# The first block of a streaming row sum, loaded in two halves by two queues

## The chip, the cores and the metric

The kernel runs on one core of a Trainium2 chip. SyncE, VectorE and ScalarE are engines of the core, each with its own stream of instructions. SyncE and ScalarE can issue loads; a load waits in the queue of the engine that issued it, and 16 DMA engines carry it out in packets. The metric is the device time of one execution in microseconds (us), as the median of several runs. The kernel before took 162.17 us in three runs.

## The reference

```python
x = np.random.randn(32, 512, 1024).astype(np.float32)   # 67.1 MB
return (np.sum(x, axis=-1) * 0.5).astype(np.float32)    # 16,384 sums
```

Each of the 16,384 rows of 1024 numbers is summed and halved. Every byte of the input is read once, and there is very little arithmetic per byte.

## The kernel before

The rows are spread over 128 partitions, 128 rows to each, and worked on in eight blocks of 16 rows (8.39 MB a block). Three buffers hold blocks in the on-chip memory. SyncE issues all loads, VectorE sums a block with one instruction, and in the last two blocks ScalarE takes some of the rows.

```python
x_pool = ctx.enter_context(tc.tile_pool(name="x", bufs=3))
...
for b in range(n_blocks - 1):
    c0 = b * B
    t = x_pool.tile([P, B, D], fp32, name="xb")
    loads.append(nc.sync.dma_start(out=t, in_=x_rows[:, c0 : c0 + B, :]))
    h = B if b < n_blocks - 2 else B // 2
    nc.vector.reduce_sum(
        out=sums[:, c0 : c0 + h], in_=t[:, 0:h, :], axis=mybir.AxisListType.X
    )
    nc.vector.tensor_single_scalar(           # sums * 0.5 -> res
        ...
    )
    for r in range(h, B):
        act_row(t, r, c0 + r)
# ... the last block comes in five pieces, and its rows are shared out ...
```

A hook that runs when the program is complete moves SyncE's first loads in front of the entry barrier, where all engines meet before their work begins. With three buffers, these are the loads of blocks 0, 1 and 2. Each later load waits for the reduction that frees its buffer.

```python
def start_loads_at_entry(nc_):
    entry, *rest = nc_.main_func.blocks
    is_sp = lambda i: i.engine == mybir.EngineType.SP
    ...   # collect SyncE's leading loads that wait for nothing
    entry.instructions = head[:at] + lead + head[at:]
```

## Time and profile before

| what | value | from |
|---|---|---|
| span of the profiled run | 160.2 us | page |
| DMA engines, share of 16 engines' span | 97.4% | page, table of queues |
| VectorE busy | 119.3 us (74%) | page |
| start of the first, second, third reduction | 21.78, 41.11, 60.46 us | timeline |
| start of the very last VectorE sum | 157.55 us | chain |

The table is read in this order. The share of the DMA engines says that the transfers never rest. The starts of the reductions say how fast blocks arrive (19.3 us apart), and the first start says what is lost before the stream has its pace. What remains of the span after the last sum is the store of the last results.

The chain that ended last, in order of time, shows the same from the back. Its columns are start, duration and piece, and "..." stands for pieces that are left out:

```profile
0.43 40.66 DMA xb<-in_x_dram
...
41.11 17.23 DVE sums L96
...
58.36 40.78 DMA xb<-in_x_dram
...
118.24 39.23 DMA xb<-in_x_dram
...
157.55 0.45 DVE xb L80
```

Each DMA piece lasts 40 us although a block takes 19.3 us. A load lies in the queue behind another one for half of that time. So a reduction that is "on the chain" does not mean that the transfers waited for it.

### The profile page before, as it was taken

How to read it: one execution, taken by the hardware profiler on the slowest of the kernel's cores; microseconds unless marked ns; L12 is line 12 of the kernel's file. 1: busy time of each engine (PE TensorE's matmuls, PEld its weight loads, DVE VectorE, ACT ScalarE, POOL GpSimd, SP SyncE). 2: the span in 40 equal slices, each digit the busy share in tenths (PEclk: the TensorE clock that was granted, in tenths of full speed). 3: DMA queues.
4: the chain of work that ended last, by engine and by line, in shares of the span. 5: the costliest groups of instructions: out<-in, count | busy, mean ns of one | idle time of the engine just before them, and what ended most of it. 6: DMA issues, size and time to landing. Idle time of an engine off the chain costs nothing.

```text
span 160.2 us, 138 instructions
## 1 busy us (share of the span) xinstructions
DVE 119.3 (74%) x34; ACT 17.3 (11%) x31; POOL 0.2 (0%) x4
## 2 busy tenths in 40 slices
DVE  0000059997799969999599995999959999597443
ACT  0000000000000000000000000000000000599952
POOL 0000000000000000000000000000000000000000
DMA  7996996996996996997997998979969969999992
GB/s 278 507 524 262 524 524 262 524 524 262 524 524 262 524 524 262 524 475 311 524 442 344 524 409 376 524 311 475 524 278 507 524 278 507 393 393 425 430 399 72
DMA packets 2016, 67.18 MB, mean 419 GB/s; under 512 B 480, under 2 KB 608, under 8 KB 736
## 3 DMA queue, kind: packets, MB, share of 16 engines
q1 hardware_dynamic: 2016, 67.18, 97.4%
HBM read 67.11 MB, written 0.07 MB: 419 GB/s over the span
## 4 chain that ended last, share of the span: by engine, by line
DMA 75%; DVE 22%; SPq 1%; issue 0%; DVEq 0%
DMA xb<-in_x_dram 75%; DVE sums L96 22%; SPq L114 1%; DVE xb L80 0%; SPq L120 0%; SPq L94 0%; DVE res L99 0%; DVEq L205 0%
## 5 line engine op out<-in xcount | busy, mean ns | idle before, releaser
L96 DVE TENSOR_REDUCE sums<-xb 128x16 f32<-128x16384 f32 (+1 forms) x7 | 112.0, 16001 | 33.3 <-DMA xb<-in_x_dram 33.3
L70 ACT ACT_TABLE_LOAD x1 | 1.3, 1283 | 137.9 <-DMA xb<-in_x_dram 137.9
L70 ACT ACTIVATE xb<-xb 128x1024 f32<-128x1024 f32 x15 | 15.7, 1045 | 2.1 <-DMA xb<-in_x_dram 2.1
L80 DVE CUSTOM_DVE_ANT_0 xb<-xb 128x512 f32<-128x512 f32 (+1 forms) x9 | 5.6, 664 | 5.0 <-DMA xb<-in_x_dram 5.0
L70 ACT ACTIVATION_READ_ACCUMULATOR xb<-xb 128x1 f32 x15 | 2.8, 187 | 0.0
L99 DVE TENSOR_SCALAR res<-sums 128x16 f32<-128x16 f32 (+1 forms) x7 | 1.2, 174 | 0.2
L80 DVE DVE_READ_ACCUMULATOR2_ANT res<- 128x1 f32 x9 | 0.7, 83 | 0.0
L80 DVE CUSTOM_DVE_ANT_0 xb<-xb,part 128x224 f32<-128x224 f32 x1 | 0.5, 450 | 0.2 <-DMA xb<-in_x_dram 0.2
L191 POOL MEMSET const-bfloat16-1.0<- 128x1 bf16 x1 | 0.1, 101 | 0.0
L191 POOL MEMSET const-uint8-127<- 128x1 uint8 x1 | 0.1, 101 | 0.0
L191 POOL MEMSET const-float32-0.0<- 128x1 f32 x1 | 0.1, 98 | 0.2 <-issue 0.2
L191 POOL MEMSET const-float32-1.0<- 128x1 f32 x1 | 0.1, 98 | 0.0
L80 DVE DVE_READ_ACCUMULATOR2_ANT part<- 128x1 f32 x1 | 0.1, 83 | 0.0
## 6 DMA issues: line engine op xcount, KB each, us to landing
xb<-in_x_dram SPq DMA_DIRECT2D x1, 4096.0 KB, 31.1
xb<-in_x_dram SPq DMA_DIRECT2D x1, 2560.0 KB, 36.9
xb<-in_x_dram SPq DMA_DIRECT2D x1, 1024.0 KB, 38.9
xb<-in_x_dram SPq DMA_DIRECT2D x1, 288.0 KB, 39.1
xb<-in_x_dram SPq DMA_DIRECT2D x1, 224.0 KB, 39.2
xb<-in_x_dram SPq DMA_DIRECT2D x7, 40.8
out_dram<-res SPq DMA_DIRECT2D x1, 56.0 KB, 10.0
out_dram<-res SPq DMA_DIRECT2D x1, 8.0 KB, 1.4
```

Of the source, the lines that this page charges most:

```text
L70: acts.append(nc.scalar.activation(out=t[:, r, :], in_=t[:, r, :], func=mybir.ActivationFunctionType.Copy, scale=mul, accum_out=res[:, col ...
L80: return nc.vector.tensor_tensor_reduce(out=t[:, r, lo:mid], in0=t[:, r, lo:mid], in1=t[:, r, mid:hi], scale=mul, scalar=start, op0=ADD, o ...
L96: nc.vector.reduce_sum(out=sums[:, c0 : c0 + h], in_=t[:, 0:h, :], axis=mybir.AxisListType.X)
L99: nc.vector.tensor_single_scalar(out=res[:, c0 : c0 + h], in_=sums[:, c0 : c0 + h], scalar=mul, op=mybir.AluOpType.mult,)
L114: nc.sync.dma_start(out=t[:, lo:hi, :], in_=x_last[:, lo:hi, :])
L191: nc = _bacc.Bacc("TRN2", target_bir_lowering=False, num_devices=1)
```

## The change

The intent is to start the stream sooner: half of the first block is issued by ScalarE, whose queue stood idle, at the same time as SyncE issues the other half. Both go in front of the barrier.

```diff
     for b in range(n_blocks - 1):
         c0 = b * B
         t = x_pool.tile([P, B, D], fp32, name="xb")
-        loads.append(nc.sync.dma_start(out=t, in_=x_rows[:, c0 : c0 + B, :]))
+        if b == 0:
+            m = B // 2
+            loads.append(nc.sync.dma_start(out=t[:, 0:m, :], in_=x_rows[:, 0:m, :]))
+            loads.append(nc.scalar.dma_start(out=t[:, m:B, :], in_=x_rows[:, m:B, :]))
+        else:
+            loads.append(nc.sync.dma_start(out=t, in_=x_rows[:, c0 : c0 + B, :]))
...
+        for engine in (mybir.EngineType.SP, mybir.EngineType.Activation):
+            start_loads_of(nc_, engine)
+
+    def start_loads_of(nc_, engine):
         entry, *rest = nc_.main_func.blocks
-        is_sp = lambda i: i.engine == mybir.EngineType.SP
+        is_own = lambda i: i.engine == engine
...   # the rest of the hook uses is_own in place of is_sp
```

More of the change, by code (lines that the diff above doesn't have):

```diff
@@ L156, in start_loads_at_entry @@
             body = list(block.instructions)
-            own = [i for i in body if is_sp(i)]
+            own = [i for i in body if is_own(i)]
             if not any(is_load(i) for i in own):
@@ L168, in start_loads_at_entry @@
             at = next(
-                k for k, i in enumerate(head) if is_sp(i) and type(i).__name__ == "InstDrain"
+                k for k, i in enumerate(head) if is_own(i) and type(i).__name__ == "InstDrain"
             )
```

## The prediction

> **What bounds the kernel now.** I read the page first (busy shares, DMA queues, chain), then the timeline of VectorE, then the DMA view of the first 4 us, then the SyncE queue's waits.
>
> The page says that the transfers never rest, while VectorE has a quarter of the span free:
>
> ```profile
> DVE 119.3 (74%) x34; ACT 17.3 (11%) x31; POOL 0.2 (0%) x4
> ...
> q1 hardware_dynamic: 2016, 67.18, 97.4%
> ...
> DMA 75%; DVE 22%; SPq 1%; issue 0%; DVEq 0%
> ```
>
> The chain names VectorE for 22%, but that is how the walk back goes (a load waits for the reduction that frees its buffer), not a time in which the queue was empty. The timeline of VectorE settles it:
>
> ```profile
> 21.78 17.22 DVE L96 TENSOR_REDUCE sums<-xb 128x16 f32<-128x16384 f32 x1 [21.78 <-DMA xb<-in_x_dram]
> 39.03 0.17 DVE L99 TENSOR_SCALAR res<-sums 128x16 f32<-128x16 f32 x1
> 41.11 17.22 DVE L96 TENSOR_REDUCE sums<-xb 128x16 f32<-128x16384 f32 x1 [1.91 <-DMA xb<-in_x_dram]
> 58.37 0.17 DVE L99 TENSOR_SCALAR res<-sums 128x16 f32<-128x16 f32 x1
> 60.46 17.22 DVE L96 TENSOR_REDUCE sums<-xb 128x16 f32<-128x16384 f32 x1 [1.91 <-DMA xb<-in_x_dram]
> ```
>
> A block is 128 x 16384 x 4 bytes = 8.39 MB. The second lands 19.33 us after the first, the third 19.35 us after the second: 8.39 MB / 19.34 us = 434 GB/s. VectorE needs 17.22 + 0.17 us for it and waits 1.91 us for the next. Eight such blocks at 19.34 us are 154.7 us of the 160.2 us span. What is left is a head, 21.78 - 19.34 = 2.44 us before the stream runs at its pace, and about 3 us of tail. The head is the only thing that a change of the first load's issue can shorten.
>
> The DMA view of the first 4 us (40 slices of 0.1 us, bytes counted where a packet begins) shows the head:
>
> ```profile
> GB/s 0 0 0 0 0 0 0 0 0 0 2621 1966 0 655 655 655 655 1311 1966 0 0 0 0 0 0 0 0 0 0 0 0 0 0 0 0 0 0 0 0 655
> DMA packets 17, 1.11 MB, mean 279 GB/s; under 512 B 0, under 2 KB 0, under 8 KB 0
> ```
>
> One packet is 64 KB (1.11 MB / 17), which in a slice is 655 GB/s. So the 16 engines begin their first packet between 1.0 and 1.9 us: 4 + 3 + 1 + 1 + 1 + 1 + 2 + 3 packets. The second round begins only at 3.9 us. In the head, 1.0 us is the way from issue to the first packet, up to 0.9 us the spread over the engines, and some 0.5 us is not resolved here (landing and signal, or a slow first packet).
>
> **What the Trainium skill says.** Four places, all in "DMA: Bandwidth & Descriptors".
> - Section "Issuing engines are not separate DMA queues": transfers issued by ScalarE and SyncE run on the same 16 engines and interleave; issuing from several "will only save the time on the sequencer it takes to initiate the DMA". The trace shows how small that time is: an issue takes 0.33 to 0.43 us. Interleaving itself is not to be seen here, since all is on one queue.
> - Section "Queues, rings and completion order": each DMA engine goes round-robin between the rows that have work, packet by packet. Nothing in this trace tests it; I use it for how the halves share the time.
> - Section "Where 436 GB/s comes from": 435.2 GB/s as the ceiling of the 16 ports. The measured 434 agrees; the stream stands within 0.3% of it, so a second queue cannot make it faster.
> - Section "Latency and other measured facts": first byte about 0.6 us after issue. Here the first packet begins at 1.0 us; the measurement decides.
>
> **The change part by part.**
> 1. *Issues.* SyncE keeps three issues before the barrier: half a block, then blocks 1 and 2. ScalarE gets one. Three issues took 1.33 us on SyncE (its first line in the timeline ends there), one on ScalarE should take about 0.4 us and begin within some 0.2 us. ScalarE thus reaches the barrier before SyncE does. Nothing waits for the barrier anyway: VectorE has no data until 21.78 us, and ScalarE's first work is at 137.9 us. Cost on the path: 0.
> 2. *First packets.* A 32 KB packet begins no earlier than a 64 KB one: the issue on SyncE is still at 0.00. Per engine, the first block was 8 packets of 64 KB and becomes 8 + 8 of 32 KB. The bytes are the same. Cost or gain: 0, with the cases below.
> 3. *More packets.* The ceiling gives 8.39 MB / 435.2 = 19.28 us a block against 19.34 measured, so the overhead of 8 packets is about 0.06 us (an estimate from that section and the row above). Eight more per engine: +0.06 us, once.
> 4. *Landing of block 0.* The reduction is still one instruction over 16 rows, so it waits for both halves; no half is used early. If the queues share evenly, both land together at 8.39 MB worth of stream: 21.8 us. If ScalarE's queue starts late, SyncE's half ends first and the last packets of ScalarE's alternate with 64 KB packets of block 1, each 19.34 / 8 = 2.42 us. One to two of those would put the landing at 24 to 27 us.
> 5. *Is that landing on the path?* The reduction of block 0 frees the buffer for block 3, whose load is issued at 39.03 us, while blocks 1 and 2 keep the queue busy until about 60.4 us: 21 us of slack. VectorE also gets back 1.91 us a block. A landing up to 5 us late is made good before block 4 and touches no transfer. Cost on the path: 0.
> 6. *Later waits.* The order of instructions on each engine is otherwise the same; the load of block 3 waits for one semaphore more, of a load long done. The five last loads are issued at 116.4 us against data wanted from 138 us on. Cost: 0.
>
> Sum: 162.17 + 0 + 0 + 0.06 = 162.2 us. I put 162.3, because of the rivals that can shift it by tenths more cost than give.
>
> **The rivals.**
> - *The head gets shorter.* Two queues may make descriptors side by side, so that every engine has work sooner. For it: the 0.9 us of spread over the engines. Against: the first packet's 1.0 us stays, and engines begin with the first half as before. It could give back half the spread, 0.4 us: 161.8. Even the whole head of 2.44 us is 1.5%, so this way alone cannot reach 2%.
> - *The head gets longer.* If both issues pass through one descriptor generator, ScalarE's descriptors can stand among SyncE's and the last engine starts up to 0.9 us later: 163.1. As every engine has the same bytes and no spare time, what the slowest one loses is never won back. For it: the starts one after another in the slices; against: an engine that has one row's packet is busy 1.2 us with it, which covers most of the gap.
> - *Changing between queues costs.* In one queue the second round begins at 3.9 us, and I do not know how much of a packet's start overlaps the one before it. If each change of row lost 0.2 us of overlap, 16 packets would be 3.2 us: 165.4, slower by 2%. For it: two streams from different places in memory. Against: large packets, and two rows with work offer more to overlap, not less. I give this 4 in 100.
> - *VectorE becomes the bound.* It would have to start 20 us late. Ruled out by the slack in 5.
>
> **Range and chances.** The three runs of before lie within 0.2 us. The head's rivals give -0.4 to +0.9 us, so 161.7 to 163.1 should hold it 8 times in 10; of the rest, more lies above, from changing queues. Faster by over 2% (under 159.0) is more than the head contains: 1 in 100. Slower by over 2% (over 165.4): 4 in 100. Within 2%: 95 in 100.
>
> **What would show it.** Right: a second queue with 4.2 MB in the table of queues; the total share of the DMA engines within 1% of now; VectorE's second to seventh reductions still 19.3 us apart and each within 0.9 us of where they were; ScalarE's issue below 0.5 us and before SyncE's third. Step 4 shows in when the first reduction starts: 21.8 us if the sharing is even, 24 to 27 us if ScalarE's half comes last, with the second reduction then only some tenths after the first. The head's rivals show in the second reduction's start, 41.11 us now, moved by the same amount as the end. I am wrong if the first block's load and the second together take over 3 us longer than 41.1 us, if a later load is issued so late that the queue runs dry, or if the end moves while the starts of the reductions do not.

## The result, and the profile after

The changed kernel took 162.12 us (median of 6 runs, 162.05 to 162.23), the kernel before 162.09 us beside it (6 runs, 161.99 to 162.18). The ratio is 1.0003 with a 95% interval of 0.999 to 1.0016, so the time is the same within the noise; the forecast 0.06 us, or 0.1 us with the tenth added for the rivals, is too small for these runs to tell from nothing. Here and below, a ratio is the mean time of one kernel's runs over the mean of the other's in the same rounds, and so not quite the ratio of the medians quoted. Executions over 1.5% slower than the fastest of the same kernel are left out of the means.

The timeline of the changed kernel's start (start, duration, engine, line, operation; in brackets the idle time before it):

```profile
0.00 0.38 SPq L97 DMA_DIRECT2D xb<-in_x_dram  x1
0.12 0.36 ACTq L98 DMA_DIRECT2D xb<-in_x_dram  x1
...
22.01 17.22 DVE L102 TENSOR_REDUCE sums<-xb 128x16 f32<-128x16384 f32 x1 [22.01 <-DMA xb<-in_x_dram]
39.26 0.18 DVE L105 TENSOR_SCALAR res<-sums 128x16 f32<-128x16 f32 x1
41.20 17.22 DVE L102 TENSOR_REDUCE sums<-xb 128x16 f32<-128x16384 f32 x1 [1.76 <-DMA xb<-in_x_dram]
...
60.55 17.22 DVE L102 TENSOR_REDUCE sums<-xb 128x16 f32<-128x16384 f32 x1 [1.92 <-DMA xb<-in_x_dram]
```

ScalarE's issue really came early, 0.12 us after SyncE's. Still, the first reduction starts at 22.01 us (21.78 before), the second and third 0.09 us later than before, and the last sum at 157.62 us (157.55 before). From the second reduction on nothing has changed but these tenths.

The table of queues in the page:

```profile
q1 hardware_dynamic: 2016, 62.98, 91.5%
q10 hardware_dynamic: 144, 4.19, 6.1%
```

The second queue carried its 4.19 MB, and the DMA engines' share is 91.5 + 6.1 = 97.6% in total, against 97.4%.

The DMA view from 2.6 to 4.0 us shows how the two queues share:

```profile
DMA packets 17, 0.56 MB, mean 398 GB/s; under 512 B 0, under 2 KB 0, under 8 KB 0
...
q10 hardware_dynamic: 16, 0.52, 86.5%
q1 hardware_dynamic: 1, 0.03, 5.4%
```

The 16 engines have each just finished one packet of SyncE's. In this stretch 16 packets of ScalarE's queue (q10) begin, one for each engine, and the first of SyncE's next round only at its end. Between 2 and 12 us each queue begins 64 packets, 2.10 MB. The sharing is strictly in turn.

### The profile page after: what moved, and what is told of

It reads as the page before. It is cut to its first block, busy times and chain, and to the rows that moved or that the text cites. A ratio compares the mean times of both kernels' runs of the same rounds, so it can differ in the third digit from the quotient of the medians.

```text
span 160.3 us, 140 instructions
## 1 busy us (share of the span) xinstructions
DVE 119.3 (74%) x34; ACT 17.3 (11%) x31; POOL 0.2 (0%) x4
## 3 DMA queue, kind: packets, MB, share of 16 engines
q1 hardware_dynamic: 2016, 62.98, 91.5%
q10 hardware_dynamic: 144, 4.19, 6.1%
## 4 chain that ended last, share of the span: by engine, by line
DMA 75%; DVE 22%; SPq 1%; issue 0%; DVEq 0%
DMA xb<-in_x_dram 75%; DVE sums L102 22%; SPq L120 1%; DVE xb L81 0%; SPq L126 0%; SPq L97 0%; DVE res L105 0%; DVEq L215 0%
## 6 DMA issues: line engine op xcount, KB each, us to landing
xb<-in_x_dram SPq DMA_DIRECT2D x2, 4096.0 KB, 26.5
```

## The experiments

**Theory A.** The stream of bytes is at its ceiling from the first packets to the last, and which queue feeds it makes no difference. Only the head (from the issue to a full stream) could be shortened, and two queues don't shorten it. **Rivals.** B: two queues do shorten the head, and changing between them eats the gain. C: the early part of the span is not on the path at all. D: the change gave nothing because the reduction waits for both halves. E to H concern the sharing and the slack and are told where they come up.

### Both halves on one queue

```diff
-            loads.append(nc.scalar.dma_start(out=t[:, m:B, :], in_=x_rows[:, m:B, :]))
+            loads.append(nc.sync.dma_start(out=t[:, m:B, :], in_=x_rows[:, m:B, :]))
```

> Both halves of block 0 on SyncE's queue, nothing on ScalarE's. Theory A (the stream is at its ceiling, which queue feeds it doesn't matter, an extra packet costs about 0.008 us): as the changed kernel, span 160.2 to 160.4 us, time within 0.1 us of the kernel before plus 0.06; the first half lands near 12 us, the second near 21.8 us, the first reduction starts at 21.8 to 22.0 us. Theory B (two queues shorten the head, and the alternation of queues eats the gain): the end comes 0.2 us or more earlier or later than the 162.12 us of the changed kernel.

Measured: 162.03 us, against 162.03 us for the kernel before beside it (ratio 1.0001, interval 0.9988 to 1.0013). The first two reductions:

```profile
21.78 17.22 DVE L102 TENSOR_REDUCE sums<-xb 128x16 f32<-128x16384 f32 x1 [21.78 <-DMA xb<-in_x_dram]
...
41.06 17.22 DVE L102 TENSOR_REDUCE sums<-xb 128x16 f32<-128x16384 f32 x1 [1.85 <-DMA xb<-in_x_dram]
```

Theory A holds and B falls by its own measure: the time is 0.09 us from that of the changed kernel, and the second queue shortened nothing. Whether it makes the head a little longer (41.20 against 41.06 us here) is taken up under the rivals at the end.

### Seven blocks in halves, by two queues and by one

```diff
-        if b == 0:
-            ...
+        m = B // 2
+        loads.append(nc.sync.dma_start(out=t[:, 0:m, :], in_=x_rows[:, c0 : c0 + m, :]))
+        loads.append(nc.scalar.dma_start(out=t[:, m:B, :], in_=x_rows[:, c0 + m : c0 + B, :]))
```

> Seven blocks in halves by both queues: 56 extra 32 KB packets per DMA engine, and the engines alternate between queues nearly all the time. Theory A: 56 x 0.008 = 0.45 us more, 162.5 us (162.3 to 162.8). Theory B (changing queues costs something beyond the packet): 112 changes of queue per engine at 0.03 us or more, so over 165 us. Reductions stay 19.4 us apart under A.

The other kernel of the pair has `nc.sync` in the last line.

> The same 32 KB packets as with both queues, all on SyncE's queue. Theory A: the same 162.5 us (162.3 to 162.8), within 0.15 us of the run with two queues. Theory B: 162.5 us here, and the run with two queues clearly above it.

Measured: 162.64 us with two queues and 162.58 us with one, against 162.03 us before (ratios 1.0037, interval 1.0024 to 1.0051, and 1.0033, interval 1.002 to 1.0046). The second and third reductions, with two queues and then with one:

```profile
41.77 17.22 DVE L99 TENSOR_REDUCE sums<-xb 128x16 f32<-128x16384 f32 x1 [2.21 <-DMA xb<-in_x_dram]
61.22 17.22 DVE L99 TENSOR_REDUCE sums<-xb 128x16 f32<-128x16384 f32 x1 [2.14 <-DMA xb<-in_x_dram]
```

```profile
41.28 17.22 DVE L99 TENSOR_REDUCE sums<-xb 128x16 f32<-128x16384 f32 x1 [2.00 <-DMA xb<-in_x_dram]
60.71 17.22 DVE L99 TENSOR_REDUCE sums<-xb 128x16 f32<-128x16384 f32 x1 [2.00 <-DMA xb<-in_x_dram]
```

In both, the second to the sixth reduction start 19.43 us apart (119.51 - 41.77 and 119.00 - 41.28, each over 4), against (118.51 - 41.11) / 4 = 19.35 us before. Eight packets more for each engine, and one more signal (the small packet that reports an engine's share of a load as done), cost 0.08 us a block, or 0.010 us for each of the eight; the signal's part in it was not measured apart. Alternating between queues adds nothing to it. The profiled run with two queues was the slowest of its five (162.97 us), and its blocks land half a microsecond later from the first on. The medians differ by 0.06 us, so I read nothing from that offset.

### The loads behind the barrier

```diff
-    nc.at_finalize(start_loads_at_entry)
```

> The kernel before with its first three loads left behind the entry barrier (at about 1.7 us). Theory A (the head is on the path one to one; later slack of VectorE and buffers makes nothing good): the first load is issued 1.7 us later, the first and second reductions start 1.7 us later (23.5 and 42.8 us), and the time is 163.8 us (163.5 to 164.1). Rival C (the early part of the span is not on the path, which would also explain that the change did nothing): 162.1 to 162.4 us.

Measured: 162.84 us against 162.03 us (ratio 1.005, interval 1.0036 to 1.0063). This kernel is the one before with that line taken out. The start of its timeline:

```profile
0.73 58.76 SPq L94 DMA_DIRECT2D xb<-in_x_dram  x5
22.57 17.22 DVE L96 TENSOR_REDUCE sums<-xb 128x16 f32<-128x16384 f32 x1 [22.57 <-DMA xb<-in_x_dram]
...
41.92 17.22 DVE L96 TENSOR_REDUCE sums<-xb 128x16 f32<-128x16384 f32 x1 [1.92 <-DMA xb<-in_x_dram]
```

My size was wrong: I took 1.7 us for the barrier from the kernel before, where SyncE issues three loads first, until 1.33 us, and so probably arrives late. Without them the loads are issued at 0.73 us. But the rule holds: the issue is 0.73 us later, the first reduction 0.79, the second 0.81, the last sum 0.83 (158.38 against 157.55) and the time 0.81. The head is on the path one to one, and rival C falls. The change had something to gain here, and gained nothing because it doesn't shorten the head.

### Two small reductions, with two queues and with one

```diff
-        nc.vector.reduce_sum(
-            out=sums[:, c0 : c0 + h], in_=t[:, 0:h, :], axis=mybir.AxisListType.X
-        )
+        for lo, hi in ((0, B // 2), (B // 2, B)) if b == 0 else ((0, h),):
+            nc.vector.reduce_sum(
+                out=sums[:, c0 + lo : c0 + hi], in_=t[:, lo:hi, :], axis=mybir.AxisListType.X
+            )
```

> Changed kernel with the reduction of block 0 as two of 8 rows. Theory A: no gain for VectorE, because even sharing lets both halves land at the same time: the first small reduction starts at 21.8 us, as before, and the time is 162.1 us (162.0 to 162.3). Rival D (the change gave nothing because the reduction waits for both halves): the first small reduction starts at about 12 us and the time falls.

> Both halves on SyncE's queue and two reductions of 8 rows. Theory A: the first half lands at about 12 us, the first small reduction starts there, 10 us earlier than before, the second at 21.9 us; VectorE is thus 8.6 us ahead after block 0, and the time is still 162.1 us (162.0 to 162.3), since the stream sets the end. Rival D: VectorE's earlier start frees buffers earlier and the time falls by 1 us or more.

Measured: 162.29 us with two queues, against 162.11 us before (ratio 1.0013, interval 0.9998 to 1.0028: not told apart from 1), and 162.07 us with one (ratio 0.9997, interval 0.9982 to 1.0012). The first reductions with two queues, then with one (the first line there is the pair of 8 rows, merged):

```profile
21.98 17.28 DVE L103 TENSOR_REDUCE sums<-xb 128x8 f32<-128x8192 f32 x2 [21.98 <-DMA xb<-in_x_dram]
```

```profile
12.10 8.69 DVE L103 TENSOR_REDUCE sums<-xb 128x8 f32<-128x8192 f32 x1 [12.10 <-DMA xb<-in_x_dram]
21.81 8.69 DVE L103 TENSOR_REDUCE sums<-xb 128x8 f32<-128x8192 f32 x1 [1.02 <-DMA xb<-in_x_dram]
...
41.15 17.22 DVE L103 TENSOR_REDUCE sums<-xb 128x16 f32<-128x16384 f32 x1 [10.45 <-DMA xb<-in_x_dram]
```

Two queues that share in turn let both halves land at the end of the block, so splitting the reduction is no use with them. The four runs of the kernel with two queues (162.18 to 162.51 us) all lie above the four with one (161.99 to 162.12 us). One queue delivers the first half 9.7 us earlier than the second. VectorE then does finish block 0 at 30.5 us in place of 39.0 us, waits 10.45 us for block 1, and the time stays the same. Rival D falls: even an early use of the first half is worth nothing, as VectorE doesn't set the end.

### ScalarE's half issued late

```diff
-        for engine in (mybir.EngineType.SP, mybir.EngineType.Activation):
+        for engine in (mybir.EngineType.SP,):
```

> Changed kernel, but ScalarE's half is issued behind the entry barrier, at about 1.7 us in place of 0.12. Theory A: SyncE's queue runs alone until the other comes in at some 2.7 to 3.4 us, so ScalarE's last packets stand behind one 64 KB packet of block 1 on at least some engines: first reduction at 23 to 25 us, second within 0.1 us of 41.2 us, end unchanged, 162.1 us (162.0 to 162.3). Rival C (the landing of block 0 is on the path): the time grows by as much as the first reduction is late, 163 to 165 us.

Measured: 162.09 us against 162.11 us (ratio 0.9999, interval 0.9984 to 1.0013). The end is unmoved, as theory A has it, but block 0 was far later than I expected, and so was the second reduction: it starts at 46.40 us and not near 41.2, since VectorE is still busy with block 0. By the fifth (99.22 us against 99.16 before) VectorE has caught up.

```profile
1.72 0.37 ACTq L98 DMA_DIRECT2D xb<-in_x_dram  x1
29.06 17.22 DVE L102 TENSOR_REDUCE sums<-xb 128x16 f32<-128x16384 f32 x1 [29.06 <-DMA xb<-in_x_dram]
```

There are two causes, both in the DMA views. From 1.0 to 5.3 us, all 49 packets that begin are SyncE's (q1), and not one is of the queue issued at 1.72 us:

```profile
q1 hardware_dynamic: 49, 1.61, 102.6%
```

Two engines begin ScalarE's first packet between 5.3 and 6.2 us and the other fourteen between 6.2 and 7.0 us, each after three or four packets of SyncE's. When SyncE's half had landed (19.3 us after its issue), ScalarE still had packets left on every engine, and each now took turns with a 64 KB packet of block 1. The last of them shows in the stretch from 28.0 to 29.1 us:

```profile
DMA packets 30, 1.05 MB, mean 953 GB/s; under 512 B 14, under 2 KB 14, under 8 KB 14
...
q1 hardware_dynamic: 16, 1.05, 219.8%
q10 hardware_dynamic: 14, 0.00, 0.7%
```

The 14 packets on q10, of 4 bytes each in the trace, are the ends of ScalarE's load, the signals of its engines; the other two engines' signals begin at about 26 us. (The share over 100% comes from counting packets whole where they begin.) No packet at all begins from 26.5 to 28.0 us: the engines are then busy with 64 KB packets of block 1, and the signals come only when these are done. So the signal takes its turn too. In all, three such packets at 2.42 us, 7.3 us, came before the landing on these 14 engines, which is 29.06 - 21.78.

### Block 1 by ScalarE's queue: how much slack is there?

```diff
-        loads.append(nc.sync.dma_start(out=t, in_=x_rows[:, c0 : c0 + B, :]))
+        queue = nc.scalar if b == 1 else nc.sync
+        loads.append(queue.dma_start(out=t, in_=x_rows[:, c0 : c0 + B, :]))
```

This and the next kernel are the one before, with the hook for both queues.

> Kernel before with the whole of block 1 issued by ScalarE at entry; blocks 0 and 1 then share the stream. Theory A (queues share by packet, and the slack before the queue runs dry is about 21 us): blocks 0 and 1 land together at 40.5 to 41.5 us, the first reduction starts about 19 us late, VectorE is then busy without a pause until the last block and gains 1.95 us a block; the load of block 3 is issued at 58.5 us, 2 us before the queue is empty, so the stream doesn't stop; VectorE ends about 1 to 2 us late, 163 to 164.5 us. Rival E (sharing is not even, or a queue goes first): block 0 lands before 35 us. Rival F (the slack is smaller than I read): the stream stops, and the time rises by over 4 us.

Measured: 164.15 us against 162.11 us (ratio 1.0122, interval 1.0105 to 1.0138). The time lies in the range, but not by the mechanism that I gave. These lines of the timeline show the first reductions, the issues from that of block 3 on, and ScalarE's first work, which waits for block 6:

```profile
41.30 34.34 DVE L98 TENSOR_REDUCE sums<-xb 128x16 f32<-128x16384 f32 x2 [41.30 <-DMA xb<-in_x_dram]
58.55 34.65 SPq L96 DMA_DIRECT2D xb<-in_x_dram  x3
...
139.93 1.28 ACT L71 ACT_TABLE_LOAD   x1 [139.93 <-DMA xb<-in_x_dram]
```

The sharing was even (rival E falls): block 0 landed together with block 1 at 41.3 us. But block 6 landed at 139.93 us, 2.0 us later than in the kernel before (137.93 us), and ScalarE waits for nothing else there. So the stream itself lost 2 us. Between 56 and 68 us it began 4.72 MB of packets, against 5.24 MB in the kernel before. The load of block 3 had been issued 1.9 us before 60.46 us, where block 2 lands in the kernel before, and that was not early enough. So rival F had the mechanism right (the stream stops), though not the size.

Where the 2 us went is seen in slices of 0.1 us, in which bytes are counted where a packet begins. These are the stretches from 58 to 62 us and from 62 to 66 us in the kernel before:

```profile
GB/s 0 0 0 0 0 0 0 0 0 0 0 0 0 0 0 655 0 1311 3932 1966 2622 0 0 0 0 0 0 0 0 0 0 0 0 0 0 0 0 0 0 0
GB/s 655 1311 3277 2621 2621 0 0 0 0 0 0 0 0 0 0 0 0 0 0 0 0 0 0 0 655 655 3932 1966 3277 0 0 0 0 0 0 0 0 0 0 0
```

And the same two stretches here:

```profile
GB/s 0 0 0 0 0 0 0 0 0 0 0 0 0 0 0 0 0 0 0 656 1311 1966 1311 0 655 655 1311 0 0 655 1311 0 0 655 0 0 0 0 0 0
GB/s 0 0 0 0 0 0 0 0 655 1311 1966 1311 655 1966 0 0 655 0 0 655 0 655 0 0 655 0 0 0 0 0 0 0 655 655 2621 1311 0 2621 0 0
```

In the kernel before, block 3's first packets begin between 59.5 and 60.1 us and its second ones between 62.0 and 62.5 us. Here the first ones begin between 59.9 and 61.4 us, 1.4 to 2.8 us after the issue, and the second ones between 62.8 and 64.5 us. The slowest engine is then 2.0 us behind, which is the loss.

### Most of block 1 by ScalarE's queue

```diff
+        if b == 1:
+            m = B - 2
+            loads.append(nc.scalar.dma_start(out=t[:, 0:m, :], in_=x_rows[:, c0 : c0 + m, :]))
+            loads.append(nc.sync.dma_start(out=t[:, m:B, :], in_=x_rows[:, c0 + m : c0 + B, :]))
+        else:
+            loads.append(nc.sync.dma_start(out=t, in_=x_rows[:, c0 : c0 + B, :]))
```

> As the run with block 1 on ScalarE's queue, but only 14 of its 16 rows (56 KB packets), the other two rows on SyncE's behind block 0. In the earlier run the load of block 3 was issued at 58.55 us, 1.9 us before the queue would be empty, and yet the engines paused and block 6 landed 2.0 us late. Theory G (a load must be issued a whole head, about 2.4 us, before the queue is empty; so the slack of block 0's landing is about 19 us and not 21): here blocks share 64 to 56, block 0 lands at about 38.7 us, 17 us late, its reduction ends and the load of block 3 is issued at 56.1 us, over 4 us before the queue is empty; no pause, block 6 lands at 137.9 to 138.2 us, and the time is 162.1 us (162.0 to 162.4). Rival H (two full queues, or VectorE without a pause, slow the stream itself): the time rises here too, by 1.5 us or more.

Measured: 162.18 us against 162.10 us (ratio 1.0005, interval 0.9989 to 1.0022). The timeline:

```profile
38.76 34.34 DVE L102 TENSOR_REDUCE sums<-xb 128x16 f32<-128x16384 f32 x2 [38.76 <-DMA xb<-in_x_dram]
...
138.06 1.28 ACT L71 ACT_TABLE_LOAD   x1 [138.06 <-DMA xb<-in_x_dram]
```

Block 0 landed 17.0 us late, and the load of block 3 was issued at 56.01 us, 4.4 us before block 2 is in. VectorE then worked without a wait into the last block as in the run before, and the time did not move. Rival H falls with that. 17.0 us late costs nothing, 19.5 us late costs 2.0 us, so the slack of block 0's landing ends between the two, as theory G says. But G's figure, a whole head of 2.44 us, is not shown: an issue 1.9 us ahead would then have cost 0.5 us, and it cost 2.0. By the slices above, the slowest engine began 2.8 us after the issue, and the engines were done with block 2 at 59.6 to 60.3 us by their signals in the trace. An estimate from these is that the load has to be issued by about 57.4 us, 3 us before 60.46 us, which leaves about 18 us of slack. No run tested a lead between 1.9 and 4.4 us.

None of the nine kernels points to a version that beats both.

## Why the prediction was right, and where a step was not

The prediction said 162.3 us, and 162.12 us was measured. Its steps sum to 162.2 us from 162.17 us for the kernel before; the further tenth, added for the rivals, had no step behind it and did not come. Beside 162.09 us for the kernel before, the change itself is 0.03 us, less than the noise.

- **Bound.** Right. The late and early landings of block 0, from 10 us early (its first half) to 17 us late, left the end alone, and a load issued 0.73 us later moved the end by 0.83 us.
- **Step 1, issues.** Right: ScalarE's issue ran from 0.12 to 0.48 us, well before SyncE's third ended. Nothing waited for it.
- **Step 2, first packets.** Right: they begin at 1.0 us as before, and the second reduction, which tells when two blocks are in, moved by 0.09 us. Five profiles with the same head (before, after, both halves on one queue, and the two with small reductions) have that start between 41.06 and 41.34 us, so 0.09 us is within their spread.
- **Step 3, more packets.** Right in kind; the term was a little small: 0.010 us a packet was measured where the working gave 0.008. For eight packets that is 0.08 us in place of 0.06. It was measured on the kernels with seven blocks in halves; in the changed kernel alone it can't be seen.
- **Step 4, landing.** Right for the changed kernel: even sharing, 22.01 us. But the worst case, "one to two of those", was too mild. In the run with ScalarE's half late, 14 engines met three 64 KB packets, since that queue joined the busy engines late and its signal took a turn as well.
- **Step 5, slack.** The conclusion was right, and the figure was wrong. "21 us of slack" counted up to the moment where the queue is empty. A load issued 1.9 us before that is too late, because it has a head of its own. By the two runs on either side the slack is between 17.0 and 19.5 us; about 18 is the estimate above.
- **Rivals.** Shorter head and longer head: neither showed beyond the spread of 0.3 us. A shorter head is refuted so far as the runs go, a longer one is not: in all three pairs that differ in the queue alone, the second reduction starts later with two queues (41.20 against 41.06 us, 41.34 against 41.15, 41.77 against 41.28), and in the two pairs that ran side by side the median times differ the same way (by 0.22 and 0.06 us). Three single profiles a side don't show that the queues do it; if they do, it is the rival of the longer head, with a few tenths at most. "Changing between queues costs": refuted, as the two kernels with seven blocks in halves have the same 19.43 us a block. My doubt whether packets overlap is answered by that as well, as far as it matters here.

The prediction left part of the head unresolved (1.0 us to the first packet, up to 0.9 us of spread, some 0.5 us of something else), and the trace of the kernel before resolves it. Its DMA view from 2 to 6 us, again in slices of 0.1 us, has the second packets of the 16 engines:

```profile
GB/s 0 0 0 0 0 0 0 0 0 0 0 0 0 0 0 0 0 0 0 655 0 1311 3277 2621 2621 0 0 0 0 0 0 0 0 0 0 0 0 0 0 0
```

They begin between 3.9 and 4.5 us, closer together than the first ones (1.0 to 1.9 us): the engines that began first had the longest first packets, up to 3.3 us by the records of single packets, where a later one takes 2.42 us. So the slowest engine is 4.5 - 2.42 = 2.1 us late after one packet. Seven more packets at 2.42 us end at 21.4 us, and 0.3 us later the reduction starts. Together that is the 2.4 us. Why the first packets last longer stays open, and no run shortened the head.

## What to carry to other kernels

Where one stream of transfers stands at its ceiling, as here at 434 GB/s, expect nothing from a second queue (seven blocks in halves took 162.64 us with two and 162.58 us with one); look for the time before the stream is full (2.4 us here), and check whether the change shortens that time or only fills it differently. Two queues share packet by packet, so two halves land together at the end, while one queue delivers them one after the other: for an early first piece, put it first on one queue. Count slack up to the moment where the next load must be issued, which is before the queue is empty: 1.9 us before was too late here, 4.4 us before was early enough.

## What the Trainium skill lacked or had wrong

- "DMA: Bandwidth & Descriptors", "Queues, rings and completion order": turns by packet are confirmed (64 to 64 packets between 2 and 12 us). The section gives 9 to 17 descriptors as typical for a packet; these traces show no descriptors, but the unit of sharing was a partition's whole run of 32, 56 or 64 KB, so a queue with 32 KB packets beside one with 64 KB gets fewer bytes.
- The same section doesn't say how long a queue waits that joins busy engines. None of its packets had begun 3.6 us after its issue (5.3 - 1.72), where idle engines began 1.0 us after it.
- "Anatomy of one DMA — SWDGE (gpsimd) path" in the same page, on transfers that GpSimd issues, puts about 100 ns on the semaphore update. For the load that ScalarE issued here, on shared engines, the signal also waited its turn behind a 64 KB packet, which takes 2.42 us.
- "Latency and other measured facts" has 0.6 us to the first byte. Counted from the start of the issue it was 1.0 us here; counted from its end (1.0 - 0.38) it was 0.6 us, so the two agree if the page counts from the issue's end, which it doesn't say.
- "Bandwidth", in the note above its table of measured loads, names about 10.5 ns a packet, to explain the floor of a 4 KB transfer issued by GpSimd. What was measured here, 0.010 us for each 32 KB packet more on every engine, is of that size; no run shows that it is the same cost.
- No page says how long before its queue is empty a load must be issued: 1.9 us ahead cost 2.0 us here, 4.4 us ahead cost nothing.
